# Two queues for the transfers of a feed-forward: moving the side traffic of the first gated ConvFFN from SyncE to GpSimd

## The chip, the cores and the metric

The kernel runs on one core of one Trainium2 chip. The time is the device time of one execution in microseconds (us). Engines: PE (TensorE), DVE (VectorE), ACT (ScalarE), POOL (GpSimd) and SP (SyncE, which here only issues transfers). Each engine runs its own instructions in order and waits on semaphores; a transfer that an engine issues stands in that engine's order like any other instruction.

## The reference, cut to what matters

One step of a two-layer encoder over 1024 prompt frames and 64 sample frames (1088 columns, width 1024). Layer 0 mixes with windowed attention, layer 1 with an S5 state-space model; each is followed by a gated convolutional feed-forward of width 2816:

```
def conv_ffn(h, prev, w_up, conv_w, conv_b, w_down):
    up = h @ w_up                                   # (t, 2*2816)
    full = concat([prev, up])                       # two rows of history
    c = conv_b + sum_j conv_w[j] * full[:, j:j+t]   # causal, width 3
    y = (gelu(c[..., :2816]) * c[..., 2816:]) @ w_down
    return y, full[:, -2:]

for i in range(2):
    x = x + rms_norm(mixer_i(rms_norm(x, g_pre_mix[i])), g_post_mix[i])
    x = x + rms_norm(conv_ffn(rms_norm(x, g_pre_ffn[i]), ...), g_post_ffn[i])
```

All is float32 at the interface. The state-space mixer of layer 1 needs tables made of its parameters alone (powers of the discretised poles, input and output matrices, a Toeplitz kernel per group); they depend on no activation and can be made at any time before layer 1.

## The kernel before, in words

Activations lie with the width on the 128 partitions and time along the rows, in three blocks of 384, 384 and 320 columns. A float32 product is three PE products of split operands (`mm3`, lines 235 to 237: low part times weight, high part times weight, high part times the weight's low part). A weight piece of 128x1024 is loaded by SP into a place called `raw` (line 196 or 213), and split by ACT and DVE into a `whl` tile (lines 198/199 and 227); `raw` has four places, `whl` six.

The first feed-forward (`ffn(0, ...)`) goes over 22 pairs of unit tiles (a gate tile and a value tile of 128 units each). A unit tile is 72 products, about 12 us of PE: three blocks `mm` of 24 products in PSUM, each read by DVE into `u` (lines 427, 429). ACT and DVE then do the convolution (`t`, lines 435 to 437), the gate is applied (line 453), and the gated pair goes to `gd` in DRAM (lines 454, 455). The down products that follow use a seven-product scheme, so they need sums of four quarters of the down weights and of the gated units. These are made beside the up-projection: `sums_w(k)` loads two pieces of `w_down` into the tile `jt` (line 368), makes four sums on DVE (371 to 374) and stores them to `sd` (375); `sums_g(k)` loads the pairs k and k+11 of `gd` into `jt` (380), makes four sums (383, 387 to 389) and stores them to `td` (390).

After each unit tile comes an `aside`: it lets one step of the side work run, and then the sums that are due by the table `starts`. The side work (`ssm_prep`) makes the tables of layer 1, in a small part and eight chunks (0 to 7). A chunk makes `ct` on DVE (lines 1055 to 1060, through the scratch tile `m`, one place), the product `w` on DVE (902 to 907 with DVE as engine), `kps` on PE (eight small products from `ct`, line 1083, each a pair in the trace), `kt` from it (1087, 1088), transposes `wps` of `w` on PE (1097) copied to `b3` (1098), a table `tab` on POOL (902 to 907 with POOL as engine, then 1106; it uses `m` too), and by way of the scratch `kd` in DRAM a Toeplitz tile `tl` (eight small loads, line 1118) and `tp` (1121). What is made is stored to `prm` (lines 1064, 1099, 1108, 1122).

The order on each engine is not the order of the code. A scheduler with a simulated timeline takes the recorded instructions, whose priority follows the place in the program, and side work has a lower one; what it decides is then fixed, and the engines run it in order. So an edit of which engine issues a transfer, or of which step it belongs to, can move any instruction near it.

Around the edit: up to the change all of these transfers but the tables' (line 1108) are issued by SP, in one order with the weight loads. In the second feed-forward (`ffn(1, ...)`), the same `sums_w`, `sums_g` and stores of `gd` are already issued by POOL, through tiles called `jw` and `jg`.

Of the kernel before, what the change touches and what calls it, by code (L numbers as in the profile page):

```python
# [8 lines left out]
F32 = mybir.dt.float32  # L9
# [6 lines left out]
P = 128  # L16
D = 1024
# [17 lines left out]
KH = KF // 2  # L35
# [8 lines left out]
class Core:  # L44
# [138 lines left out]
    def load_unit(self, src):  # L183
        nc = self.nc
        raw = self.wts.tile([P, D], F32, name="raw", tag="raw", bufs=4)
# [167 lines left out]
    def ffn(self, i, h, rb, after, side=None, beside=lambda: None, x=None, g=None):  # L353
# [10 lines left out]
        E, Q = nc.vector, (nc.sync, nc.gpsimd)[i]  # L364
# [12 lines left out]
        def sums_g(k):  # L377
            x = jt[:, :1536] if i == 0 else ts.tile([P, 1536], F32, name="jg", tag="t2")
            x = x.rearrange("p (c b t) -> p c b t", c=2, b=2)
            Q.dma_start(x, gd[:, k::KH, :768].rearrange("p c (b t) -> p c b t", b=2))  # L380
            yield
            a11, a12, a21, a22 = x[:, 0, 0], x[:, 0, 1], x[:, 1, 0], x[:, 1, 1]
            v = E.tensor_sub(a11, a12, a11)
# [11 lines left out]
        starts.update({2 * (k + KH) + 3 - i: sums_g(k) for k in range(KH)})  # L395
        jobs = {}

        def sums(j):
# [638 lines left out]
    def ssm_chunk(self, q):  # L1037
# [26 lines left out]
        nc.sync.dma_start(self.prm[:, gs, OC:OC + 256], oc.rearrange("p g c i t -> p g (c i t)"))  # L1064
# [6 lines left out]
        w = self.jt[:, 2048:].rearrange("p (g c j s) -> p g c j s", g=4, c=2, j=16)  # L1071
# [17 lines left out]
        nc.sync.dma_start(self.kd[q * P:q * P + P, 7:].rearrange("j t i -> j (t i)"), kt)  # L1089
# [9 lines left out]
        nc.sync.dma_start(self.prm[:, gs, OW:OW + 256], b3.rearrange("p g c n -> p g (c n)"))  # L1099
# [10 lines left out]
    def ssm_toeplitz(self, q):  # L1110
# [11 lines left out]
        nc.sync.dma_start(self.prm[:, 4 * q:4 * q + 4, OKT:OKT + 256], tp.rearrange("p (g e) f -> p g (e f)", e=2))  # L1122
# [105 lines left out]
    def ssm(self, after):  # L1228
# [4 lines left out]
        with tc.tile_pool(name="ss", bufs=1) as sp:  # L1233
# [36 lines left out]
            def batch(qs):  # L1270
# [11 lines left out]
                if e0 == 0:  # L1282

                    sc = self.wts.tile([P, D], F32, name="sc", tag="raw", bufs=4) if t < 8 or t == 9 else self.yp.tile([P, D], F32, name="sc", tag="ypA", bufs=2)
# [348 lines left out]
```

## Time and profile before

| | |
|---|---|
| runs | 2238.78, 2240.88, 2244.19 us; median 2240.88 |
| profiled execution | 2242.71 us, span 2240.9 us, mean clock of PE 0.989 |
| PE busy | 2192.9 us, 98% of the span |
| DVE busy | 1656.4 us, 74% |
| ACT, POOL busy | 1041.0 us, 46%; 410.0 us, 18% |
| first up-projection | about 383 to 929 us of the span |
| down products of layer 0 | about 929 to 1120 us |

The groups of the profile show what waits: ACT's splits wait for PE to free a `whl` place, PE hardly ever waits for a weight.

```profile
L227 ACT ACTIVATE whl<-raw 128x1024 fp32r<-128x1024 f32 x201 | 210.4, 1057 | 220.1 <-PE mm L237 193.7
L235 PE MATMUL mm<-hl,whl 128*128 128x384 f32 (+1 forms) x1960 | 643.7, 329 | 5.9 <-DVE hl L319 4.0
```

A line of this kind is a group of instructions: line, engine, operation, tile written and tiles read, count, then busy us and mean ns, then the engine's idle time just before them and what ended most of it.

### The profile page before, as it was taken

What the parts mean: (1) busy time and instruction counts of PE and PEld (TensorE: products, weight loads), DVE (VectorE), ACT (ScalarE), POOL (GpSimd) and SP (SyncE); (2) the same over time, 40 slices, a digit from 0 to 9 for tenths busy, and PEclk for the clock granted to TensorE, in tenths of its full rate; (3) what the DMA queues carried; (4) which work ended last, traced back from release to release, by engine and by line L of the source; (5) the groups of instructions that cost most, each with busy time, mean ns of one, the idle gap of its engine ahead of it and who ended that gap; (6) DMA issues with size and microseconds to landing.
All of it is one profiled execution on the core that took longest, in us unless ns stands there. A gap on an engine that the chain in (4) does not pass through costs nothing. (4 is left out here: it accounts for less than half of the span.)

```text
span 2240.9 us, 35962 instructions
## 1 busy us (share of the span) xinstructions
PE 2192.9 (98%) x13875; PEld 2119.2 (95%) x13875; DVE 1656.4 (74%) x2887; ACT 1041.0 (46%) x1895; POOL 410.0 (18%) x470
## 2 busy tenths in 40 slices
PE   9999999999999999999999899999999999999997
PEld 8987799999999999999996799999999999999997
DVE  8688648999778777766768855598976777677764
ACT  6256756322243333555545642263554445455553
POOL 5222005100032423100200034352010110100000
PEclk9999999999999999999999899999999999999999
DMA  6000015655245655886749988652266786578772
GB/s 221 32 30 21 20 62 170 229 212 201 95 147 181 191 184 167 285 290 212 240 154 342 284 282 301 239 167 75 91 233 216 260 274 208 194 252 316 224 267 73
DMA packets 208123, 428.47 MB, mean 191 GB/s; under 512 B 23312, under 2 KB 114224, under 8 KB 205008
## 3 DMA queue, kind: packets, MB, share of 16 engines
q1 hardware_dynamic: 175648, 326.56, 43.0%
q0 software_dynamic: 23984, 95.12, 11.9%
q10 hardware_dynamic: 8320, 4.49, 0.9%
q8 instruction: 109, 1.79, 0.3%
q14 instruction: 62, 0.51, 0.1%
HBM read 297.75 MB, written 128.37 MB: 190 GB/s over the span
## 5 line engine op out<-in xcount | busy, mean ns | idle before, releaser
L235 PE MATMUL mm<-hl,whl 128*128 128x384 f32 (+1 forms) x1960 | 643.7, 329 | 5.9 <-DVE hl L319 4.0
L236 PE MATMUL mm<-hh,whl 128*128 128x384 f32 (+1 forms) x1960 | 644.2, 329 | 0.0
L237 PE MATMUL mm<-hh,whl 128*128 128x384 f32 (+1 forms) x1960 | 642.8, 329 | 0.6 <-DVE whl L227 0.5
L235 PEld LDWEIGHTS mm<-hl,whl 128*128 128x128 f32 x1960 | 369.3, 189 | 8.1 <-DVE hl L319 4.9
L237 PEld LDWEIGHTS mm<-hh,whl 128*128 128x128 f32 x1960 | 369.3, 189 | 1.5 <-DVE whl L227 0.8
L236 PEld LDWEIGHTS mm<-hh,whl 128*128 128x128 f32 x1960 | 369.5, 189 | 0.2
L227 DVE TENSOR_TENSOR whl<-raw,whl 128x1024 fp32r<-128x1024 f32 x201 | 254.9, 1275 | 99.5 <-ACT whl L227 97.0
L235 PE MATMUL mm<-gt,whl 128*128 128x384 f32 (+1 forms) x968 | 316.4, 327 | 0.1
L236 PE MATMUL mm<-gt,whl 128*128 128x384 f32 (+1 forms) x968 | 316.0, 327 | 0.0
L237 PE MATMUL mm<-gt,whl 128*128 128x384 f32 (+1 forms) x968 | 315.5, 326 | 0.0
L227 ACT ACTIVATE whl<-raw 128x1024 fp32r<-128x1024 f32 x201 | 210.4, 1057 | 220.1 <-PE mm L237 193.7
L235 PEld LDWEIGHTS mm<-gt,whl 128*128 128x128 f32 x968 | 181.7, 188 | 0.4 <-DVE y L626 0.4
L236 PEld LDWEIGHTS mm<-gt,whl 128*128 128x128 f32 x968 | 181.7, 188 | 0.0
L237 PEld LDWEIGHTS mm<-gt,whl 128*128 128x128 f32 x968 | 181.7, 188 | 0.0
L199 DVE TENSOR_TENSOR whl<-raw,whl 128x1024 fp32r<-128x1024 f32 x84 | 95.7, 1152 | 54.0 <-ACT whl L198 53.9
L436 DVE SCALAR_TENSOR_TENSOR t<-u,ppt,t 128x1090 f32<-128x1090 f32 x88 | 126.2, 1435 | 5.5 <-ACT t L435 4.9
L435 ACT ACTIVATE t<-u,ppt 128x1090 f32<-128x1090 f32 x88 | 114.1, 1297 | 23.4 <-DVE u L532 13.0
L437 DVE SCALAR_TENSOR_TENSOR t<-u,ppt,t 128x1090 f32<-128x1090 f32 x88 | 123.3, 1403 | 0.5
L198 ACT ACTIVATE whl<-raw 128x1024 fp32r<-128x1024 f32 x84 | 82.2, 984 | 88.8 <-PE mm L237 88.0
L427 DVE TENSOR_TENSOR u<-rb,mm 128x384 f32<-128x384 f32 (+1 forms) x164 | 80.9, 503 | 47.8 <-PE mm L237 41.5
L576 DVE TENSOR_TENSOR gt<-gr,gt 128x768 fp32r<-128x768 f32 (+2 forms) x106 | 89.8, 872 | 27.9 <-ACT gt L575 27.6
L575 ACT ACTIVATE gt<-gr 128x768 fp32r<-128x768 f32 (+2 forms) x106 | 78.4, 771 | 53.1 <-DMA gr<-gd 24.7
(390 smaller groups left out, 4109.7 us busy)
## 6 DMA issues: line engine op xcount, KB each, us to landing
raw<-in_w_up SPq DMA_DIRECT2D x88, 512.0 KB, 4.4
raw<-in_w_down SPq DMA_DIRECT2D x74, 512.0 KB, 4.8
raw<-sd SPq DMA_DIRECT2D x40, 512.0 KB, 4.6
sj<-in_w_up POOLq DMA_DIRECT2D x68, 256.0 KB, 6.1
su<-sj POOLq DMA_DIRECT2D x34, 512.0 KB, 5.9
raw<-su SPq DMA_DIRECT2D x34, 512.0 KB, 3.8
pm<-prm SPq DMA_DIRECT2D x32, 522.0 KB, 7.7
gr<-td SPq DMA_DIRECT2D x40, 384.0 KB, 6.2
```

Source lines behind the costliest of these rows:

```text
L198: nc.scalar.activation(w[:, 0], raw, AF.Copy)
L199: nc.vector.tensor_sub(w[:, 1], raw, w[:, 0].bitcast(F32))
L227: x = nc.scalar.activation(w[:, 0], raw, AF.Copy), nc.vector.tensor_sub(w[:, 1], raw, w[:, 0].bitcast(F32))
L235: nc.tensor.matmul(out, w[:, 0, sl], xl, start=start, stop=False, skip_group_check=more)
L236: nc.tensor.matmul(out, w[:, 0, sl], xh, start=False, stop=False, skip_group_check=more)
L237: self.last_mm = nc.tensor.matmul(out, w[:, 1, sl], xh, start=False, stop=stop, skip_group_check=more)
L427: nc.vector.tensor_mul(u[:, t0 + 2:t0 + 2 + np_], rb[:, t0:t0 + np_], ps[:, :np_])
L435: nc.scalar.activation(t, u[:, 0:T + 2], AF.Identity, bias=cb(m), scale=cw(0, m))
L436: nc.vector.scalar_tensor_tensor(t, u[:, 1:T + 3], cw(1, m), t, op0=ALU.mult, op1=ALU.add)
L437: self.last_conv = nc.vector.scalar_tensor_tensor(t, u[:, 2:T + 4], cw(2, m), t, op0=ALU.mult, op1=ALU.add)
L575: nc.scalar.activation(x[:, 0, u], raw, AF.Copy)
L576: nc.vector.tensor_sub(x[:, 1, u], raw, x[:, 0, u].bitcast(F32))
```

## The change

Three things are edited.

1. In `ffn(0)` the queue `Q` is GpSimd's instead of SyncE's. The loads and stores of `sums_w` and `sums_g` and the stores to `gd` are issued by POOL, and in `ssm_chunk` and `ssm_toeplitz` so are the stores to `kd` and `prm` and the loads of `tl`. In all 185 transfers leave SP. The weights, the inputs of the norms and layer 1's loads stay on SP.
2. `sums_g(k)` loads at aside 2(k+11)+2 instead of 2(k+11)+3, and its sums are made two asides after the load instead of one. Two of them can now be under way, so they use the two halves of `jt` in turn; the tile `w` of the chunks, which lay in the third part of `jt`, gets a tile of its own.
3. `raw` (and the tile `sc` of layer 1, which has the same tag) has three places instead of four. The room goes to `w`.

```
-        raw = self.wts.tile([P, D], F32, name="raw", tag="raw", bufs=4)
+        raw = self.wts.tile([P, D], F32, name="raw", tag="raw", bufs=3)
...
-        E, Q = nc.vector, (nc.sync, nc.gpsimd)[i]
+        E, Q = nc.vector, nc.gpsimd
...
         def sums_g(k):
-            x = jt[:, :1536] if i == 0 else ts.tile([P, 1536], F32, name="jg", tag="t2")
+            x = jt[:, k % 2 * 1536:k % 2 * 1536 + 1536] if i == 0 else ts.tile([P, 1536], F32, name="jg", tag="t2")
...
-        starts.update({2 * (k + KH) + 3 - i: sums_g(k) for k in range(KH)})
+        starts.update({2 * (k + KH) + 2: sums_g(k) for k in range(KH)})
         jobs = {}
         def sums(j):
...
             if j in starts:
                 x = starts[j]
                 next(x)
-                jobs[j + 1 + i] = [x]
+                jobs.setdefault(j + 1 + (i or j > 2 * KH), []).append(x)
...
         if q == 0:
-            nc.sync.dma_start(self.kd[:, 0:7].rearrange("(b p) t i -> p b (t i)", p=P), z)
+            nc.gpsimd.dma_start(self.kd[:, 0:7].rearrange("(b p) t i -> p b (t i)", p=P), z)
...
-        nc.sync.dma_start(self.prm[:, gs, OC:OC + 256], oc.rearrange("p g c i t -> p g (c i t)"))
+        nc.gpsimd.dma_start(self.prm[:, gs, OC:OC + 256], oc.rearrange("p g c i t -> p g (c i t)"))
...
-        w = self.jt[:, 2048:].rearrange("p (g c j s) -> p g c j s", g=4, c=2, j=16)
+        w = self.prep2.tile([P, 4, 2, 16, 8], F32, name="w")
...
-        nc.sync.dma_start(self.kd[q * P:q * P + P, 7:].rearrange("j t i -> j (t i)"), kt)
+        nc.gpsimd.dma_start(self.kd[q * P:q * P + P, 7:].rearrange("j t i -> j (t i)"), kt)
...
-        nc.sync.dma_start(self.prm[:, gs, OW:OW + 256], b3.rearrange("p g c n -> p g (c n)"))
+        nc.gpsimd.dma_start(self.prm[:, gs, OW:OW + 256], b3.rearrange("p g c n -> p g (c n)"))
...
         for s in range(8):
-            nc.sync.dma_start(dst, src)
+            nc.gpsimd.dma_start(dst, src)
...
-        nc.sync.dma_start(self.prm[:, 4 * q:4 * q + 4, OKT:OKT + 256], tp.rearrange("p (g e) f -> p g (e f)", e=2))
+        nc.gpsimd.dma_start(self.prm[:, 4 * q:4 * q + 4, OKT:OKT + 256], tp.rearrange("p (g e) f -> p g (e f)", e=2))
```

The scheduler then sets another order at many places. Three are shown. The first is DVE at the start of the up-projection, where the last block's normed input is split into `hl` (line 319; the numbers behind names tell tiles apart, `jt` is the tile of the weight sums). Before:

```order
L372 TENSOR_TENSOR jt_4586<-jt_4586 128x512
L302 TENSOR_TENSOR nvsqb_3937<-nvsqb_3937 128x3
L344 TENSOR_TENSOR q_512<-q_512,xl_3847 128x640
L265 TENSOR_TENSOR sqb_3972<-sqb_3972,sqb_3974 128x640
L373 TENSOR_TENSOR jt_4586<-jt_4586 128x512
L303 TENSOR_TENSOR nvsqb_3937<-nvsqb_3937 128x3
L319 SCALAR_TENSOR_TENSOR hl_3949<-q_512,ppt_91,hh_3948 128x320 x2
L374 TENSOR_TENSOR jt_4586<-jt_4586 128x512
```

and with the change:

```order
L372 TENSOR_TENSOR jt_4586<-jt_4586 128x512
L302 TENSOR_TENSOR nvsqb_3937<-nvsqb_3937 128x3
L265 TENSOR_TENSOR sqb_3972<-sqb_3972,sqb_3974 128x640
L373 TENSOR_TENSOR jt_4586<-jt_4586 128x512
L303 TENSOR_TENSOR nvsqb_3937<-nvsqb_3937 128x3
L344 TENSOR_TENSOR q_512<-q_512,xl_3847 128x640
L374 TENSOR_TENSOR jt_4586<-jt_4586 128x512
L304 SCALAR_TENSOR_TENSOR nvsqb_3937<-nvsqb_3937 128x3
L319 SCALAR_TENSOR_TENSOR hl_3949<-q_512,ppt_91,hh_3948 128x320
L265 TENSOR_TENSOR sqb_3972<-sqb_3972,sqb_3977 128x640
L319 SCALAR_TENSOR_TENSOR hl_3949<-q_512,ppt_91,hh_3948 128x320
```

The last weight sum L374 stood behind the two last `hl`, and now stands ahead of them.

The second is DVE at the eighth chunk's `ct` (chunk 7), from the gated sum L383 on. Before:

```order
L383 TENSOR_TENSOR jt_4586<-jt_4586 128x384
L1055 TENSOR_TENSOR m_7019<-tq_4274,tp_4275 128x576
L1056 TENSOR_TENSOR m_7019<-tq_4274,tp_4275 128x576
L436 SCALAR_TENSOR_TENSOR t_8639<-u_8556,ppt_91,t_8639 128x1090
L387 TENSOR_TENSOR jt_4586<-jt_4586 128x384
L427 TENSOR_TENSOR u_8654<-rb_3688,mm_8657 128x384
L1057 TENSOR_TENSOR ct_7018<-m_7019 128x4x144
L437 SCALAR_TENSOR_TENSOR t_8639<-u_8556,ppt_91,t_8639 128x1090
```

and with the change, somewhat later in the program:

```order
L427 TENSOR_TENSOR u_8766<-rb_3688,mm_8803 128x384
L388 TENSOR_TENSOR jt_4586<-jt_4586 128x384
L1055 TENSOR_TENSOR m_7026<-tq_4274,tp_4275 128x576
L1056 TENSOR_TENSOR m_7026<-tq_4274,tp_4275 128x576
L389 TENSOR_TENSOR jt_4586<-jt_4586 128x384
L1057 TENSOR_TENSOR ct_7025<-m_7026 128x4x144
L1058 TENSOR_TENSOR m_7026<-tq_4274,tp_4275 128x576
L1059 TENSOR_TENSOR m_7026<-tq_4274,tp_4275 128x576
L427 TENSOR_TENSOR u_8774<-rb_3688,mm_8829 128x384
L1060 SCALAR_TENSOR_TENSOR ct_7025<-m_7026 128x4x144
```

The chunk's `ct` stood right behind L383, the first operation on the loaded gated units; now two blocks of `u` and most of the sums stand between. On PE the first `kps` of this chunk stood after the 20th product of `mm_8795`, with one product between each two; now it stands here, after the 18th product of `mm_8855`, and the other seven follow 14 products later, in `mm_8881`, without a product between:

```order
L236 MATMUL mm_8855<-hh_3897,whl_8561 128x384
L237 MATMUL mm_8855<-hh_3897,whl_8561 128x384
L1083 MATMUL kps_7148<-ct_7025,bd_4569 128x128
L235 MATMUL mm_8855<-hl_3898,whl_8561 128x384
L236 MATMUL mm_8855<-hh_3897,whl_8561 128x384
```

and

```order
L235 MATMUL mm_8881<-hl_3898,whl_8660 128x384
L236 MATMUL mm_8881<-hh_3897,whl_8660 128x384
L1083 MATMUL kps_7148<-ct_7025,bd_4569 128x128 x7
L237 MATMUL mm_8881<-hh_3897,whl_8660 128x384
L235 MATMUL mm_8881<-hl_3898,whl_8660 128x384
```

The third is POOL in the up-projection, at one chunk's table. Before:

```order
L902 TENSOR_TENSOR m_5814<-tq_4274,tp_4275 128x576
L903 TENSOR_TENSOR m_5814<-tq_4274,tp_4275 128x576
L904 TENSOR_TENSOR tab_5813<-m_5814 128x4x144
L905 TENSOR_TENSOR m_5814<-tq_4274,tp_4275 128x576
L906 TENSOR_TENSOR m_5814<-tq_4274,tp_4275 128x576
L907 TENSOR_TENSOR tab_5813<-m_5814 128x4x144
```

and with the change:

```order
L903 TENSOR_TENSOR m_5818<-tq_4274,tp_4275 128x576
L380 DMA jt_4586<-gd0_4001 128x2x768
L1118 DMA tp_4275<-kd_295 16x8x128 x8
L904 TENSOR_TENSOR tab_5817<-m_5818 128x4x144
L1099 DMA prm_294<-b3_5803 128x4x256
L390 DMA td0_4003<-jt_4586 128x1536
L905 TENSOR_TENSOR m_5818<-tq_4274,tp_4275 128x576
L906 TENSOR_TENSOR m_5818<-tq_4274,tp_4275 128x576
L1122 DMA prm_294<-tp_6065 128x4x256
L454 DMA gd0_4001<-t_7677 128x1024
L455 DMA gd0_4001<-t_7677 128x64
L907 TENSOR_TENSOR tab_5817<-m_5818 128x4x144
```

The table's six operations stood together; now 14 transfers stand among them behind its second one, each of which waits for what it reads.

More of the change, by code (lines that the diff above doesn't have):

```diff
@@ L1282, in batch @@
                 if e0 == 0:
-                    sc = self.wts.tile([P, D], F32, name="sc", tag="raw", bufs=4) if t < 8 or t == 9 else self.yp.tile([P, D], F32, name="sc", tag="ypA", bufs=2)
+                    sc = self.wts.tile([P, D], F32, name="sc", tag="raw", bufs=3) if t < 8 or t == 9 else self.yp.tile([P, D], F32, name="sc", tag="ypA", bufs=2)
                     tiles[t] += [sc[:, :552].rearrange("p (e c k) -> p e c k", e=2, c=2), sp.tile([P, 2, 2, 138], F32, name="rd", bufs=2)]
```

## The prediction, made before the change was run

> **What bounds the kernel now.** I read the page first, then PE by stage, then who PE waits for in the changed stage, and last the timelines around each wait.
>
> ```profile
> span 2240.9 us, 35962 instructions
> 350.00:560.00 210.00, 204.53 (x1238) 203.27 (x1237) 193.12 (x475) 81.47 (x134) 35.40 (x25) 0.98 0.61 215
> 560.00:850.00 290.00, 290.00 (x1811) 289.56 (x1810) 230.12 (x367) 105.51 (x149) 79.53 (x56) 1.00 0.50 161
> 850.00:930.00 80.00, 75.30 (x452) 74.57 (x451) 54.69 (x82) 28.31 (x40) 22.97 (x17) 0.96 0.64 210
> 930.00:1120.00 190.00, 190.00 (x1127) 189.91 (x1127) 137.54 (x176) 105.10 (x141) 14.84 (x11) 1.00 0.75 253
> ```
>
> A row is a stretch: its length, then the busy time of PE, PEld, DVE, ACT and POOL, and the granted clock of PE before the DMA share. The first feed-forward's up-projection lies between about 383 and 929 us. PE is the bound: it has no idle time at all from 560 to 850 and from 930 to 1120. Nothing that the change does there can gain; it can only lose. What can be won is PE's 5.5 us before 560, its 4.7 us after 850, and the time in which its clock was low.
>
> ```profile
> PE kps L1083 <- DVE ct L1060: 3.9, 1, 3.9
> PE mm L235 <- DVE hl L319: 3.7, 2, 2.4
> PE mm L235 <- DVE u L427: 1.8, 1, 1.8
> PE kps L1083 <- DVE ct L1057: 0.8, 1, 0.8
> 400.00:405.00 5.00, 4.11 (x18) 4.11 (x19) 4.20 (x9) 0.74 (x1) 1.95 (x2) 0.67 0.90 353
> 435.00:440.00 5.00, 5.00 (x20) 5.00 (x21) 5.00 (x10) 2.51 (x4) 0.00 (x0) 0.66 0.26 88
> 885.00:890.00 5.00, 5.00 (x22) 5.00 (x23) 5.00 (x10) 2.17 (x4) 0.00 (x0) 0.52 0.82 296
> ```
>
> These are all of PE's waits from 350 to 930 us (total, times, longest), and the stretches behind them. Each wait but the shortest is followed by some 3 to 5 us of low clock, so a wait costs itself and a slow stretch. I call them A (400 us, for `hl`), B (435 us, for `u`) and C (880 to 890 us, for the eighth chunk's `ct`). (The Trainium skill, "TensorE: Matmul & The Clock Gate", Part 1, has the clock halved after an idle window of about 3.4 us and restored after as long a busy one; the rows agree on the length of the slow stretch, but B shows it after 1.8 us.)
>
> C comes from a transfer:
>
> ```profile
> 869.73 0.57 SPq L380 DMA_DIRECT2D jt<-gd  x1
> 875.25 0.56 DVE L383 TENSOR_TENSOR jt<-jt 128x384 f32<-128x384 f32 x1 [10.11 <-DMA jt<-gd]
> 875.72 0.75 DVE L1055 TENSOR_TENSOR m<-tq,tp 128x576 f32<-128x576 f32 x1
> 876.39 0.75 DVE L1056 TENSOR_TENSOR m<-tq,tp 128x576 f32<-128x576 f32 x1
> 883.93 0.75 DVE L1060 SCALAR_TENSOR_TENSOR ct<-m 128x576 f32<-128x576 f32 x1
> 840.40 0.34 PE L235 MATMUL mm<-hl,whl 128*128 128x384 f32 x1
> 840.57 0.38 PE L1083 MATMUL kps<-ct,bd 128*128 128x128 f32 x2
> 840.97 0.38 PE L1083 MATMUL kps<-ct,bd 128*128 128x128 f32 x2
> 880.16 0.46 PE L1083 MATMUL kps<-ct,bd 128*128 128x128 f32 x2 [0.76 <-DVE ct L1057]
> 884.74 0.80 PE L1083 MATMUL kps<-ct,bd 128*128 128x128 f32 x2 [3.94 <-DVE ct L1060]
> 889.66 0.48 PE L235 MATMUL mm<-hl,whl 128*128 128x384 f32 x1
> ```
>
> The load of the gated units goes out on SP at 869.73, behind the stores it needs. DVE, in order, stands 10.1 us at L383; all of the chunk's work is queued behind it. DVE then works without a gap, but `ct` is done at 884.7, and PE has stood for it twice.
>
> **The change part by part.** Sums are made against the profiled execution, 2242.7 us (span 2240.9 and 1.8 around it); it lies 1.8 above the runs' median of 2240.88, so I take differences and set them against the median.
>
> *C goes.* The waits are 0.76 + 3.94 = 4.70. From 884.74 to 889.66 PE runs seven groups (a pair of `kps` and one product) in 4.92; in the chunk before, a group took 840.97 - 840.57 = 0.40, so seven are 2.8 and 2.1 are lost to the clock, with 0.2 at the ends. C is 7.0 in all. In the new order the load L380 is issued half a pair earlier, L383 stands behind a later `u`, and the first `kps` stands 13 rows later on PE, with the other seven 14 products behind it. A product of 384 columns takes 0.17 (840.40 to 840.57). From the end of `mm_8829`, the last block that DVE reads before L1060, to the seven `kps` there are 18 + 14 products, 5.5 us. DVE at that point: from the end of `mm_8803` it has L427, L388, L1055, L1056, L389, L1057, L1058, L1059, by the spacing in C's own timeline (875.25 to 875.72, 0.47, for a short one, and to 876.39, 0.67, for one of 576 elements) 3 x 0.47 + 5 x 0.67 = 4.8, against 24 x 0.17 = 4.2 for `mm_8829`; then L427 and L1060, 1.2. `ct` is done about 1.8 after `mm_8829` and wanted at 5.5: 3.7 us of room, where before it was 3.9 late. Should DVE come late by the whole room, C comes back step for step. C: -7.0, bounds -7.0 and 0.
>
> *A grows.* DVE's rows where its second wait (2.4 us) ends:
>
> ```profile
> 400.10 1.20 DVE L319 SCALAR_TENSOR_TENSOR hl<-q,ppt,hh 128x320 fp32r<-128x320 f32 x2
> 401.22 1.35 DVE L374 TENSOR_TENSOR jt<-jt 128x512 f32<-128x512 f32 x1
> ```
>
> The new order puts L374 ahead of the two last L319, so `hl` for k=4 comes 1.3 later: +1.3 here, bounds 0 (L374 took 0.68 where POOL did not compute beside it) and +2.5 (a longer slow stretch). POOL's third `hl` now stands behind L375, which waits for L374; PE wants it about 5 us after that, with the k=4 to 6 products and eight of the next unit before it, so it is hidden.
>
> *B shrinks a little.* `jt` has one place for the weight sums: store, load, sum.
>
> ```profile
> 415.66 0.33 SPq L375 DMA_DIRECT2D sd<-jt  x1
> 424.07 0.39 SPq L368 DMA_DIRECT2D jt<-in_w_down  x1
> 430.49 0.69 DVE L371 TENSOR_TENSOR jt<-jt 128x512 f32<-128x512 f32 x1 [0.38 <-DMA jt<-in_w_down]
> sd<-jw POOLq DMA_DIRECT2D x11, 1024.0 KB, 4.9
> jw<-in_w_down POOLq DMA_DIRECT2D x11, 1024.0 KB, 6.2
> gd<-t SPq DMA_DIRECT2D x21, 512.0 KB, 2.6
> gd<-t POOLq DMA_DIRECT2D x22, 512.0 KB, 4.5
> ```
>
> On SP the load waited 4 us behind a weight load. On POOL, with the landing times that the same transfers have in the second feed-forward, it lands at 415.7 + 0.5 + 4.9 + 0.7 + 6.2 = 428.0, so the 0.38 goes, and three small operations (0.3) have moved behind `u`: -0.7, bounds 0 and -3.5 (the 1.8 and its slow stretch, 5 x 0.34 = 1.7, all gone).
>
> *The moved transfers.* 185 issues leave SP and enter POOL's queue:
>
> ```profile
> L375 POOL DMA_DIRECT2D sd<-jw x11: 532/549/565, 1642.1 to 1828.5; - x11
> L1108 POOL DMA_DIRECT2D prm<-tab x16 | 12.4, 775 | 3.2 <-POOL tab L1106 3.1
> L907 POOL TENSOR_TENSOR tab<-m 128x576 f32<-128x576 f32 x8 | 16.0, 1998 | 0.6
> POOL m L902 <- DVE jt L907: 364.0, 8, 182.6
> ```
>
> One costs 0.55 to 0.78 of POOL where it cost SP 0.33 (415.66). A chunk (some 40 us: 840.57 to 880.16) brings eight L1118, four other small ones and about seven of the gated units: 19 x 0.55 = 10.5 to 19 x 0.78 = 15, besides the table's 12 us (six operations of up to 2.0). POOL sat idle 364 us waiting for the chunks before, so it has the time. What is queued behind a waiting issue is the table (L904 to L907), and the next chunk's L1055 on DVE needs it done, since both use `m`. In chunk 7 I count from DVE's w (its L907): L902 and L903, two issues, the wait for `b3` some 7 us on, two issues, then four operations of about 1.75: done near 15 us, against L1055 at about 23. For other chunks POOL may hold DVE by up to 3 us, about the room of their `kps`. I set 0, bounds 0 and +6 (one more event like C).
>
> *Three raw places and the second half of `jt`.* A weight piece must be loaded into the place of the third before it:
>
> ```profile
> 936.38 1.04 ACT L198 ACTIVATE whl<-raw 128x1024 fp32r<-128x1024 f32 x1
> 938.96 2.35 DVE L199 TENSOR_TENSOR whl<-raw,whl 128x1024 fp32r<-128x1024 f32 x2
> 946.28 1.06 ACT L198 ACTIVATE whl<-raw 128x1024 fp32r<-128x1024 f32 x1 [2.20 <-PE mm L237]
> raw<-in_w_down SPq DMA_DIRECT2D x22, 512.0 KB, 4.8
> ```
>
> The piece split at 936.38 is free at 940.2; the third after it is split at 946.28, which is 6.1 later, and a load lands in 4.8. ACT waited there for PE, not for the load. In the up-projection pieces come about 12 us apart. Nothing, therefore; if that cover went, the split would move by what is missing, behind six `whl` places.
>
> Sum: -7.0 + 1.3 - 0.7 = -6.4; 2240.9 - 6.4 = 2234.5 (2236.3 for an execution like the profiled one).
>
> **The rivals.**
>
> *C only moves* (no measurable change). DVE leaves the wait for `jt<-gd` and stands at L1055 or L1057 for POOL instead, with `kps` late again. For it: L1055 to L1060 are in the same order behind POOL's table, and POOL's queue has got longer. Against it: the room of 3.7 and of 8 us above. If half of C stays and A grows, 2240.9 - 3.5 + 1.3 = 2238.7; all of it, 2242.2.
>
> *POOL's queue is the new bound* (slower). One in-order queue now holds stores that wait for DVE, loads that wait for stores, and tables that DVE waits for. Each L380 stands for a `gd` store's landing, 4.5 on POOL against 2.6, and L907 stands behind them. If that makes L1055 late by more than about 3.7 in two chunks that lost nothing before, each costs a C without its first wait, 3.9 + 2.3 = 6.2: 2240.9 - 6.4 + 12.4 = 2246.9. It decides once POOL is held some 8 us longer per chunk than I count. Against it: 364 us of slack. (The Trainium skill speaks for it: "DMA: Bandwidth & Descriptors", SWDGE vs HWDGE vs iDMA, leaves plain transfers to SP or ACT, and "SBUF — State Buffer", the "DVE blocks DMA" trap, has GpSimd's descriptors starved while DVE runs certain copies. The rows of the second feed-forward show landings of up to 6.2 us on POOL and a store later by 1.9, no queue that stops.)
>
> *All three waits go* (larger gain). If the later weight sums also free DVE at A and B: 7.0 + 3.5 + 4.0 for A's second wait and its clock (2.4 and 5 x 0.33), 2240.9 - 14.5 = 2226.4. Against it, L374 ahead of `hl`.
>
> **How the numbers follow.** Forecast 0.50, C only moves 0.26, POOL's queue 0.16, all go 0.08. This kernel's measurement tells 0.2%, 4.5 us, from no change. The forecast lies only 1.9 beyond it, so a tenth of its chance falls within: faster 0.45 + 0.08 and 0.01 of the first rival = 0.54; same 0.05 + 0.25 = 0.30; slower 0.16. The range takes in the larger gain's near side and the slower case's: 2228 to 2246; the forecast's own, from its bounds, is 2231 to 2238.
>
> **What would show it.** Right: PE's waits from 350 to 930 have no `kps` row, 850 to 930 is busy for the whole of its length at clock 1.00, and DVE's wait at L383 is near nothing. A's wait is near 3.7 rather than 2.4. Wrong: a `kps` wait with DVE standing at L1055 or L1057 for POOL L907 or for the store of `b`; a low clock between 560 and 850; splits of ACT waiting for raw loads after 930.

## The result and the profile after

The changed kernel takes 2254.11 us (median of 5 runs, 2249.62 to 2256.09), the kernel before 2240.88 beside it: ratio 1.0057, 95% interval 1.0044 to 1.0069. It is slower by 13, where 6 less were forecast, and 8 above the range. Run a second time, it took 2249.88 against 2243.18 (ratio 1.0037, 1.0023 to 1.0052). Two single executions, one of the kernel before (9453 us) and the profiled one of r3_tabst below (3044 us at a granted clock of 0.65), are left out of all ratios.

Two stretches of the changed kernel that were shown of before (length; busy PE, PEld, DVE, ACT, POOL; PE's granted clock; DMA share), with two at the start of the down products:

```profile
560.00:850.00 290.00, 290.00 (x1805) 289.65 (x1804) 230.70 (x349) 104.38 (x148) 135.94 (x164) 1.00 0.50 171
850.00:930.00 80.00, 75.40 (x470) 74.95 (x469) 62.77 (x84) 29.17 (x40) 45.97 (x53) 0.98 0.62 198
925.00:930.00 5.00, 0.93 (x3) 0.96 (x4) 2.03 (x3) 2.39 (x4) 0.00 (x0) 0.70 1.05 379
930.00:935.00 5.00, 5.00 (x21) 5.00 (x20) 5.00 (x9) 4.53 (x7) 0.65 (x2) 0.62 0.65 225
```

and PE's waits from 350 to 930 us (total, times, longest):

```profile
PE mm L235 <- DVE gt L576: 4.6, 1, 4.6
PE mm L235 <- DVE u L427: 2.6, 1, 2.6
PE mm L235 <- DVE hl L319: 2.4, 1, 2.4
PE mm L235 <- DVE u L429: 0.8, 1, 0.8
```

Both `kps` rows are gone: C went. A new row stands first, the wait for `gt`, the split of the gated units that the first down products take. It ends at 929, and the clock is low to 935. So 850 to 930 has no more busy time than before, for another reason. The transfers of the eighth chunk on the way to C, now:

```profile
869.66 0.77 POOL L380 DMA_DIRECT2D jt<-gd  x1
881.63 0.55 DVE L383 TENSOR_TENSOR jt<-jt 128x384 f32<-128x384 f32 x1
889.22 0.75 DVE L1060 SCALAR_TENSOR_TENSOR ct<-m 128x576 f32<-128x576 f32 x1
889.80 0.38 PE L1083 MATMUL kps<-ct,bd 128*128 128x128 f32 x2
892.45 1.72 PE L1083 MATMUL kps<-ct,bd 128*128 128x128 f32 x14
```

L380 goes out at the same time as before (869.7), but DVE comes to L383 late enough to find it landed, and no `kps` waits. What changed is where the work stands: the chunk's first `kps` comes 9.6 later than before (880.16), of which this execution was 2.5 behind, and `ct` is done at 890.0, 2.5 before the other seven `kps`.

To see where the rest went I compare the start of the same matrix product, by its place in PE's order, in two profiled executions. The differences of the changed kernel to the one before, in us gained or lost per stretch (marks are times of the kernel before):

```
stretch             first profile   second profile
start to 700 (A, B)      +2.5           +0.5
700 to 905 (C)           -7.5           -7.5
905 to 945 (gt)          +7.0           +6.7
945 to 1530              +4.9           +2.5
1530 to 1820             +2.9           +2.5
1820 to the end          +1.2           +0.7
sum                     +11.0           +5.4
```

C gave its whole gain; the start of the down products took it back; and 6 to 9 us more were lost after 945, in stages in which the change moves no transfer. PE's waits from 950 to 2300 us, before:

```profile
PE p L1281 <- DMA pm<-prm: 3.1, 3, 2.0
PE pr L279 <- DVE sqa L273: 1.7, 1, 1.7
PE p L1341 <- ACT ys L1355: 1.5, 1, 1.5
PE mm L235 <- DVE u L531: 1.5, 2, 1.1
```

and with the change:

```profile
PE p L1281 <- DMA pm<-prm: 6.2, 3, 4.0
PE mm L235 <- DVE u L531: 5.4, 5, 1.4
PE pr L279 <- DVE sqa L273: 3.9, 2, 2.2
PE p L1341 <- ACT ys L1355: 2.8, 1, 2.8
```

The four together are 18.3 against 7.8, and with the rows not shown, some of which fell, 28.5 against 22.7: the later loss is spread over several stages.

### The profile page after: what moved, and what is told of

It reads as the page before. It is cut to its first block, busy times and chain, and to the rows that moved or that the text cites. A ratio compares the mean times of both kernels' runs of the same rounds, so it can differ in the third digit from the quotient of the medians.

```text
span 2252.3 us, 36013 instructions
## 1 busy us (share of the span) xinstructions
PE 2197.9 (98%) x13875; PEld 2122.1 (94%) x13875; DVE 1667.4 (74%) x2887; ACT 1040.7 (46%) x1895; POOL 513.7 (23%) x655
## 5 line engine op out<-in xcount | busy, mean ns | idle before, releaser
L227 DVE TENSOR_TENSOR whl<-raw,whl 128x1024 fp32r<-128x1024 f32 x201 | 258.2, 1291 | 103.1 <-ACT whl L227 102.4
L199 DVE TENSOR_TENSOR whl<-raw,whl 128x1024 fp32r<-128x1024 f32 x84 | 98.9, 1186 | 56.9 <-ACT whl L198 56.8
L436 DVE SCALAR_TENSOR_TENSOR t<-u,ppt,t 128x1090 f32<-128x1090 f32 x88 | 127.9, 1455 | 6.5 <-ACT t L435 5.7
L437 DVE SCALAR_TENSOR_TENSOR t<-u,ppt,t 128x1090 f32<-128x1090 f32 x88 | 127.3, 1448 | 0.8
L344 POOL TENSOR_TENSOR y<-y,xl 128x768 f32<-128x768 f32 (+1 forms) x16 | 30.2, 1888 | 327.9 <-DVE y L341 263.4
```

Source lines behind the costliest of these rows:

```text
L199: nc.vector.tensor_sub(w[:, 1], raw, w[:, 0].bitcast(F32))
L227: x = nc.scalar.activation(w[:, 0], raw, AF.Copy), nc.vector.tensor_sub(w[:, 1], raw, w[:, 0].bitcast(F32))
L344: x = by[q].tensor_add(yq, yq, xs[q])
L436: nc.vector.scalar_tensor_tensor(t, u[:, 1:T + 3], cw(1, m), t, op0=ALU.mult, op1=ALU.add)
L437: self.last_conv = nc.vector.scalar_tensor_tensor(t, u[:, 2:T + 4], cw(2, m), t, op0=ALU.mult, op1=ALU.add)
```

## The experiments

Two questions: what makes `gt` late at 925, and what costs after 945? In the table each row is one profiled execution against the first one of before, by the same stretches, and the ratio of all its runs to those of before on its chip. "Tables" are the six transfers of the parameter chunks (L1045, L1064, L1089, L1099, L1118, L1122), "stores" the gated units' L454 and L455, "sums" L368, L375, L380 and L390; named are those that POOL issues in the first feed-forward.

```
run         on POOL                  to 700  C      gt    later  ratio (95%)
change      all                      +2.5   -7.5   +7.0   +9.0   1.0057 (1.0044-1.0069)
r1_after    all (again)              +0.5   -7.5   +6.7   +5.6   1.0037 (1.0023-1.0052)
e2_queue    all, old start of sums   +1.6   -7.5   +3.6   +7.8   1.0077 (1.0059-1.0095)
e3_raw4     all, four raw places     +0.9   -7.4   +3.7  +10.1   1.0071 (1.0054-1.0088)
e8_gr       all and L587             -0.5   -7.5   +2.1  +13.1   1.0028 (1.0015-1.0041)
t1_pad8     all, 8 copies            -0.7   -7.5   +6.1   +1.3   1.0034 (1.0020-1.0048)
e7_prepsp   stores, sums, shifted    +3.6   -7.5    0.0   +9.0   1.0009 (0.9995-1.0023)
e6_sums     stores, sums             +2.2   -7.5    0.0   +8.7   1.0038 (1.0022-1.0054)
e10_tabst   tables, stores           +1.0   -7.5    0.0   +7.8   1.0014 (1.0000-1.0027)
e9_tabsums  tables, sums              0.0   -7.5    0.0   +3.1   0.9995 (0.9985-1.0005)
r4_tabsums  tables, sums (again)     -1.5   -7.5    0.0   +3.1   1.0004 (0.9990-1.0018)
t2_pad31    tables, sums, 31 copies  -0.3   -7.5    0.0   +4.7   1.0008 (0.9996-1.0021)
e5_prep     tables                   -0.7   -7.5    0.0   +1.9   0.9978 (0.9966-0.9990)
e1_raw3     none, three raw places   -3.5   -3.2    0.0   +2.2   0.9993 (0.9983-1.0004)
e4_shift    none, shifted sums       -1.7   +6.2    0.0   +0.1   1.0029 (1.0018-1.0040)
d1_dummy    88 more stores           -3.8  +11.2   +0.3   +2.3   1.0063 (1.0039-1.0086)
d2_dummy    44 more stores           -3.9   +2.5   +0.2   +1.7   1.0040 (1.0025-1.0055)
r2_before   none (before again)      -1.2   -0.1    0.0   -0.3   0.9996 (0.9987-1.0005)
```

### The parts of the change

Three raw places alone:

```
-  raw = self.wts.tile([P, D], F32, name="raw", tag="raw", bufs=4)
+  raw = self.wts.tile([P, D], F32, name="raw", tag="raw", bufs=3)
   (and the same for sc)
```

> The kernel before with three raw places instead of four and nothing else (all transfers still on SP, sums as before). Theory (the loss is the third edit: SP issues weight loads in order, a load that waits for its raw place holds every load behind it on SP): the eighth chunk's wait for kps stays, and the losses seen behind 905 us come: a wait for gt at the start of the down products (about +7 with its slow clock), the state-space and GLU stage (+2 to +4), the second feed-forward (+3 to +6): 2251 to 2258 us. Rival (the loss comes from GpSimd's transfers, by their descriptors or their queue): 2239 to 2244 us.

2238.29 against 2239.33: no cost. The first theory after the result, that the third place was needed, fell.

The queue alone, with the old start of the sums, four raw places and one place of `jt`:

```
-  E, Q = nc.vector, (nc.sync, nc.gpsimd)[i]
+  E, Q = nc.vector, nc.gpsimd
   (and nc.sync to nc.gpsimd in the six transfers of the tables)
```

> The first edit alone: the 185 transfers issued by GpSimd, sums_g at its old asides in one part of jt, w in jt, four raw places. Theory (raw places are the loss): nothing is lost behind 930 us; the load L380 no longer stands behind SP's weight loads, so part of the eighth chunk's wait (7.0) goes, the wait B grows by about 2.5: 2235 to 2242 us. Rival (GpSimd's transfers are the loss): 2248 to 2256 us.

2257.99 (2248.65 to 2260.78; the profiled execution is the lowest of them). The whole loss is in this part of the change: C goes, `gt` is waited for, and the later stages lose.

The change with four raw places; one place of `jt` for the gated sums, `w` in `jt`:

```
-  raw = self.wts.tile([P, D], F32, name="raw", tag="raw", bufs=3)
+  raw = self.wts.tile([P, D], F32, name="raw", tag="raw", bufs=4)
   (and the same for sc)
-  w = self.prep2.tile([P, 4, 2, 16, 8], F32, name="w")
+  w = self.jt[:, 2048:].rearrange("p (g c j s) -> p g c j s", g=4, c=2, j=16)
```

> The change with four raw places: w back in the last third of jt, so the gated sums use one place of jt in turn instead of two; queue and asides as in the change. Theory (raw places are the loss): the eighth chunk's kps waits are gone (-7), B +2.5, nothing behind 930 us: 2234 to 2238 us. Rival (GpSimd's transfers are the loss): 2248 to 2256 us.

2253.13: the fourth raw place gives nothing back.

The shift of the gated sums alone, everything on SP:

```
-  starts.update({2 * (k + KH) + 3 - i: sums_g(k) for k in range(KH)})
+  starts.update({2 * (k + KH) + 2: sums_g(k) for k in range(KH)})
-  jobs[j + 1 + i] = [x]
+  jobs.setdefault(j + 1 + (i or j > 2 * KH), []).append(x)
```

> The second edit alone: the gated sums loaded half a pair earlier and made two asides after the load, in one place of jt, all transfers on SP, four raw places. Theory: the kps waits of the eighth chunk go by the shift alone: 2233 to 2237 us. Rival (it takes the queue on GpSimd to have the load out early): the 10 us wait at L383 stays, 2239 to 2243 us.

2244.73, ratio 1.0029. The shift does not remove C by itself; it gives more such waits. PE's in the up-projection:

```profile
PE kps L1083 <- DVE ct L1060: 6.5, 3, 3.5
PE kps L1083 <- DVE ct L1057: 3.4, 1, 3.4
```

### What the queue does: each family by itself

The tables' transfers alone go to POOL:

```
-  nc.sync.dma_start(dst, src)
+  nc.gpsimd.dma_start(dst, src)
   (L1118; the same in L1045, L1064, L1089, L1099 and L1122)
```

> The kernel before with only the tables' transfers (L1045, L1064, L1089, L1099, L1118, L1122: 105 issues) on POOL's queue; the gated units' stores and the sums stay on SP, in the old order. Theory (order of transfers): POOL's last table, L906, stands behind the last chunk's eight L1118 and so frees the place for gr<-gd late: the down products begin with a wait for gt of 3 to 5 us (none before), +3 to +4 from 905 to 945 us; C stays about as large as before or gets a little smaller. Theory (later landings): jw<-in_w_down lands about 0.5 us later than before's 6.2 and the second feed-forward loses 3 to 6 us; in all 2245 to 2251. Rival (only the sums and stores carry the loss): no gt wait, second feed-forward as before, 2238 to 2243.

2234.2 against 2238.85, faster by 0.10 to 0.34%: the best of all kernels here, and against both theories, as it has no `gt` wait and loses only 1.9 later. C is gone with the sums still on SP and at their old start. The rows of the last gated unit that the load needs show why. Its operations are L436, L437 and L453 on DVE, then the stores L454 and L455. Before:

```profile
852.29 5.62 SPq L1118 DMA_DIRECT2D tp<-kd  x8
854.12 2.27 DVE L436 SCALAR_TENSOR_TENSOR t<-u,ppt,t 128x1090 f32<-128x1090 f32 x1
857.49 2.36 POOL L907 TENSOR_TENSOR tab<-m 128x576 f32<-128x576 f32 x1
858.95 2.06 DVE L453 TENSOR_TENSOR t<-t 128x1090 f32<-128x1090 f32 x1
861.99 0.38 SPq L1122 DMA_DIRECT2D prm<-tp  x1
862.46 1.86 SPq L454 DMA_DIRECT2D gd<-t  x1
869.73 0.57 SPq L380 DMA_DIRECT2D jt<-gd  x1
```

and with the tables' transfers on POOL:

```profile
850.38 4.18 POOL L1118 DMA_DIRECT2D tp<-kd  x8 [1.61 <-DMA kd<-kt]
850.56 1.35 DVE L436 SCALAR_TENSOR_TENSOR t<-u,ppt,t 128x1090 f32<-128x1090 f32 x1 [0.32 <-ACT t L435]
853.69 1.29 DVE L453 TENSOR_TENSOR t<-t 128x1090 f32<-128x1090 f32 x1
855.00 0.32 SPq L454 DMA_DIRECT2D gd<-t  x1
858.43 0.53 SPq L380 DMA_DIRECT2D jt<-gd  x1
```

The load goes out 11.3 earlier. Only 1.4 of this is SP's queue: the eight L1118 were through before the unit was made (L453 ends at 861.0), and its store then stood behind L1122 until 862.5. Another 6.0 come from DVE, where L453 now ends at 855.0. L436, L437 and L453 took 2.27, 2.15 and 2.06 before, while POOL computed its table beside them, and take 1.35, 1.36 and 1.29 here, while POOL is mostly issuing transfers; that is 2.5, and the rest is the place in DVE's order. The last 3.8 lie between store and load, which waits for the landing (7.3 before, 3.4 here). DVE's order behind the load moved too: L1055 stood right behind L383, and now comes 8 after it. So moving the tables' transfers removes C, but less by freeing SP's queue than by what it changes on POOL, on DVE and in the landing; no run changes these one at a time.

Only the sums and the stores go to POOL, old start:

```
-  E, Q = nc.vector, (nc.sync, nc.gpsimd)[i]
+  E, Q = nc.vector, nc.gpsimd
```

> The kernel before with only the gated units' stores and the two kinds of sums on POOL's queue (80 issues in the first feed-forward); the tables' transfers stay on SP, the start of the sums is unchanged. Theory (order of transfers): no gt wait at the start of the down products, because POOL's tables have no L1118 ahead of them. C: the load of the gated units goes out in the same place, but its store lands 1.9 us later (4.5 against 2.6), so C stays or grows by 2. Theory (later landings, by number of transfers): 80 of 185 moved, the second feed-forward loses some 2 to 3 us; in all 2241 to 2248. Rival: landings do not depend on what went before, second feed-forward as before, 2239 to 2243.

2246.33, no `gt` wait, C gone as well; but later +8.7. The change with the tables' transfers back on SP (shift, three raw places and the second half of `jt` stay):

```
-  nc.gpsimd.dma_start(dst, src)
+  nc.sync.dma_start(dst, src)     (and the other five)
```

> The change with the six tables' transfers back on SP; the sums and stores on POOL, the shift of the sums, three raw places and the second half of jt stay. Theory (order of transfers): C is gone (-7 by 905 us), no gt wait of more than 1 us at 925, so 945 stands at -4 to -7 against before, where the whole change stands at +2; the rest loses 2 to 4 in the second feed-forward if the earlier transfers set its landings: 2235 to 2242. Rival (any GpSimd transfer near the tables makes gr late): gt wait of 3 to 5 again and 2245 to 2252.

2241.47, not to be told from before; no `gt` wait. (Its profiled execution, the +9.0 of the table, is the slowest of its twelve, 2248.23.) So neither family makes `gt` late by itself. Of the later loss I thought that it grows with what has gone through POOL's queue before. That was tried by 88 more stores of 256 KB from POOL in the first feed-forward, to a piece of DRAM that nobody reads (it shifts the addresses of later ones):

```
+  [nc.gpsimd.dma_start(dum[:, f, j], ta[:, 128 * j:128 * j + 512])
+   for j in range(4)]              (behind L455, first feed-forward)
```

> The kernel before with 88 more POOL stores of 256 KB in the first feed-forward (four a pair), to a piece of DRAM that nobody reads; they add no work for the later stages, whose instructions keep their order on every engine. (The piece of DRAM moves the addresses of later ones.) Theory (what went through POOL's queue earlier sets later landings): jw<-in_w_down lands later than 6.2 by 0.5 or more, and the second feed-forward is 4 to 8 us longer than before though nothing in it changed: 2244 to 2252. Rival (landings depend on what runs at the time): the second feed-forward within 1 us of before, landings 6.2 to 6.4; whatever is lost is lost before 930 us.

2253.06, but the loss lies before 905 us, in three `kps` waits (11.9 in all); later +2.3, like the 2.2 of e1_raw3. That theory fell.

### Which order makes gt late

The change again, unaltered:

> The changed kernel once more, unaltered, for a second profiled execution. What belongs to the program stands again at the same place: C gone (905 us at -4 to -6 against before), the wait for gt of 3 to 5 with its slow stretch (+6 to +7 from 905 to 945), waits A and B together +2 to +3. Theory that the later losses belong to the program too: +4 at 1440 us and +1 to +3 in the second feed-forward come again, span 2250 to 2255. Rival (they are chance of one execution): they come at other places or not at all.

The `gt` wait is 4.5 and C -7.5 again; the later loss is 5.6 instead of 9.0, with nothing at 1440, where 4 had gone. The change with the first gated loads on POOL:

```
-  nc.sync.dma_start(r[:, :n], gd[:, 6 * x:6 * x + n, :384])
+  (nc.gpsimd, nc.sync)[i].dma_start(r[:, :n], gd[:, 6 * x:6 * x + n, :384])
```

> The change with one edit: the first two loads of gated units for the down products (L587, first feed-forward) are issued by POOL, right behind the last table, instead of by SP, where they stand behind two weight loads that hold the queue for 7 us. Theory (the loss at 925 us is this queue position): the loads go out near 915 instead of 917 to 924 and land by 920; the wait for gt falls from 4.6 to below 1, 945 us stands at -3 to -5 against before instead of +2, and the whole is 5 to 7 faster than the change: 2246 to 2249. Rival (the last table itself is what is late, whoever issues): gt wait stays above 3, 2252 to 2256.

The rows of SP, POOL and PE around the first gated loads L587 (`gr`); they need the place of the last chunk's tables, so L906. Before:

```profile
899.00 1.17 POOL L906 TENSOR_TENSOR m<-tq,tp 128x576 f32<-128x576 f32 x1
907.74 2.70 SPq L587 DMA_DIRECT2D gr<-gd  x2
912.96 4.65 SPq L196 DMA_DIRECT2D raw<-in_w_down  x2
```

with the change:

```profile
909.57 7.12 SPq L196 DMA_DIRECT2D raw<-in_w_down  x2
910.55 2.22 POOL L906 TENSOR_TENSOR m<-tq,tp 128x576 f32<-128x576 f32 x1
916.87 1.04 SPq L587 DMA_DIRECT2D gr<-gd  x2
927.09 2.31 ACT L575 ACTIVATE gt<-gr 128x768 fp32r<-128x768 f32 x3 [5.26 <-DMA gr<-gd]
929.07 0.66 PE L235 MATMUL mm<-gt,whl 128*128 128x384 f32 x1 [4.60 <-DVE gt L576]
```

and with L587 on POOL:

```profile
907.34 2.22 POOL L906 TENSOR_TENSOR m<-tq,tp 128x576 f32<-128x576 f32 x1
911.98 1.74 POOL L587 DMA_DIRECT2D gr<-gd  x2
918.75 2.31 ACT L575 ACTIVATE gt<-gr 128x768 fp32r<-128x768 f32 x3
```

and PE's wait there in this kernel:

```profile
PE mm L235 <- DVE gt L576: 1.9, 1, 1.9
```

In the changed order two weight loads L196 stand ahead of L587 on SP, and before they stood behind it. They hold SP until 916.7, four after L906 is done at 912.8, and the DMA engines are full while the last loads land (share 1.05 from 925 to 930). Off that queue, L587 goes out 2.4 after L906's end, the split begins 8 earlier (3 of it because this execution was ahead by then), and the stretch loses 2.1 instead of 6.7 to 7.0. The wait goes with the program's order: in the five profiles with L196 ahead (change, r1_after, e2_queue, e3_raw4, t1_pad8) PE waits 3.3 to 4.6 for `gt`, in all those with L587 ahead not at all. But the last table is late in the same five: L906 ends at 909.4 to 912.8 there, and at 908.0 at the latest in those without the wait. In the change its operations L902 to L906 take 14.7 us on POOL (898.1 to 912.8) with eleven transfers among them, before 7.2. With L587 off SP's queue PE still waits 1.9 of the 4.6. So 2.7 are shown for the two weight loads; the 1.9 stand with the late table, which no run moved by itself. It takes all three families on POOL to get that order, which two further kernels show. Tables and sums, stores on SP:

```
   before, with nc.gpsimd in the tables' six transfers
-  Q.dma_start(...)           (L368, L375, L380, L390)
+  nc.gpsimd.dma_start(...)
```

> The kernel before with the tables' transfers and those of the sums (L368, L375, L380, L390) on POOL; the gated units' stores (L454, L455) stay on SP; old start of the sums. Tables alone gave 2234.2, all three kinds together 2258.0. Theory (any wait in the one queue that the tables share with the sums makes the last table late): gt wait of 3 to 5 at 925, 2246 to 2256. Rival (it is the 44 stores in the queue, which wait for the gated units): no gt wait, 2234 to 2243.

Tables and stores, sums on SP:

```
   before, with nc.gpsimd in the tables' six transfers
-  Q.dma_start(gd[...], ta[...])           (L454, L455)
+  nc.gpsimd.dma_start(gd[...], ta[...])
```

> The kernel before with the tables' transfers and the gated units' stores (L454, L455) on POOL; the sums' transfers stay on SP. Theory (any wait in the queue that the tables share makes the last table late): stores wait for the gated unit, up to 9 us each, so gt wait of 2 to 5 and 2240 to 2250; L380 on SP waits 1.9 longer for a store that lands in 4.5, so some of C may come back. Rival (only the sums matter, whose load waits for the store of the unit before it): no gt wait, 2232 to 2238.

Neither has a `gt` wait. In both the last table is done by 904.6 (L906 at 903.43 and 897.01), and L587 stands ahead of L196. For the whole time e8_gr gains nothing, though: 2249.83 beside 2249.88 of the unaltered change; its profiled execution lost 13.1 later. The `gt` wait is shown as a loss of its stretch; a gain of the whole from shortening it is not.

### What costs after 945

By now the kernels that store the gated units from POOL lost 5.6 to 13.1 after 945, those that do not 0.1 to 3.1. The pair e9_tabsums and e10_tabst is the sharpest: from about 1260 us on they have the same instructions in the same order on every engine. The second feed-forward of e9_tabsums, at one weight sum:

```profile
1663.20 0.71 POOL L368 DMA_DIRECT2D jw<-in_w_down  x1 [5.06 <-DMA sd<-jw]
1668.26 0.55 POOL L454 DMA_DIRECT2D gd<-t  x1 [4.35 <-DVE t L453]
1668.96 0.69 DVE L371 TENSOR_TENSOR jw<-jw 128x512 f32<-128x512 f32 x1 [0.99 <-DMA jw<-in_w_down]
```

and of e10_tabst, whose products there run 0.9 ahead of it:

```profile
1666.66 0.71 POOL L368 DMA_DIRECT2D jw<-in_w_down  x1 [6.72 <-DMA sd<-jw]
1667.41 0.56 POOL L454 DMA_DIRECT2D gd<-t  x1
1676.61 0.69 DVE L371 TENSOR_TENSOR jw<-jw 128x512 f32<-128x512 f32 x1 [9.50 <-DMA jw<-in_w_down]
```

The store before lands later, so the load goes out with the gated store right behind it, and DVE stands 9.5 instead of 1.0 for it; `u` comes late and PE waits 4.7. In this execution the chain of store, load and sum has grown a small delay into a wait of PE. Was it chance, or the kernel? Before, e10_tabst and e9_tabsums again, unaltered, and before with 44 more POOL stores in the gated stores' own shapes:

```
+  [nc.gpsimd.dma_start(dum[:, f, o:e], ta[:, o + (2 if o else 0):e + (2 if o else 0)])
+   for o, e in ((0, SEQ), (SEQ, T))]      (behind L455, first feed-forward)
```

> The kernel before once more, unaltered, for a second profiled execution. Theory (the loss of 2 to 7 us between 1530 and 1820 us belongs to kernels that store the first stage's gated units from POOL): none here, within 1 us of the first. Rival (chance of an execution, whatever the kernel): it may come here too, with a wait for u L531 of 2 to 5.

> The tables' transfers and the gated units' stores on POOL once more, unaltered. Its first profiled execution lost 6.3 in one wait for u L531 near 1690 us, where the load of a weight sum went out at the same time as a store and a weight load. Theory (belongs to the kernel): 2 to 7 lost again between 1530 and 1820. Rival (chance): 0 to 1, or at another k.

> The tables' and the sums' transfers on POOL once more, unaltered. From the middle of the gated stage on, its instructions and waits are the same, engine by engine, as those of the kernel with the stores instead of the sums. Theory (belongs to the stores): 1530 to 1820 within 1 of before, again. Rival (chance): 2 to 7 lost here this time.

> The kernel before, in which POOL also writes each gated unit of the first feed-forward, in the gated stores' own two shapes (44 more transfers), to a piece of DRAM that nobody reads; SP's own stores stay. Theory (stores of these shapes through POOL's queue do something that lasts): 2 to 7 lost between 1530 and 1820. Rival (no such thing): within 1 of before there; whatever is lost is lost before 930, at the waits for kps.

r2_before and r4_tabsums lost nothing from 1530 to 1820 (-1.3 and -2.2), nor did d2_dummy (+0.7): in this execution, more stores of these shapes on POOL did nothing that lasted. It is the fastest of d2_dummy's four, 2243.62; the other three took 2246.49 to 2250.14, and where they lost it is not known. r3_tabst has no profile that can be compared by stretch; its runs gave 1.0010 (0.9994 to 1.0025).

One thing differed at the head of that chain. The sum's last operation and its store, in before (second profile):

```profile
1640.56 0.69 DVE L374 TENSOR_TENSOR jw<-jw 128x512 f32<-128x512 f32 x1
1641.55 0.53 POOL L375 DMA_DIRECT2D sd<-jw  x1 [10.43 <-DVE u L409]
```

and with the change:

```profile
1648.01 0.69 DVE L374 TENSOR_TENSOR jw<-jw 128x512 f32<-128x512 f32 x1
1649.46 0.53 POOL L375 DMA_DIRECT2D sd<-jw  x1 [10.89 <-DVE u L409]
```

POOL issues 0.30 after the sum there and 0.76 here. Such late issues, always by 0.46, stand at the same transfers in repeats. In all five profiles in which the first store was late (e2_queue, e3_raw4, e10_tabst, and the change twice) this stage lost 2.5 to 7.2 (e7_prepsp lost 3.7 and e8_gr 2.1 without one). I took them to be places in POOL's own stream, and moved them by small copies on POOL, with every other engine's order kept: off the first store in the change (8 copies), onto it in e9_tabsums (31 copies).

```
+  [nc.gpsimd.tensor_copy(pad[:, j:j + 1], ta[:, j:j + 1]) for j in range(8)]
   (behind L455, second feed-forward, first pair; 31 spread over four pairs)
```

> The change with eight copies of one column added on POOL, behind the first gated unit's stores of the second feed-forward, where POOL is idle for over 10 us; every other engine's order is the same. Theory (at fixed places in its own stream POOL starts an instruction 0.46 us late, and in the change one of these places is the store of the first weight sum, from which the chain store, load, sum comes late and grows): the places move by eight instructions, to a gated store and to waits that are idle anyway; the first store goes out 0.3 behind the sum instead of 0.75, and the second feed-forward (1530 to 1820) stands within 1 of before, where the two profiles of the change lost 2.9 and 2.5. In all 1 to 4 less than the change. Rival (the place on POOL is not the cause): 2 to 4 lost again.

> The kernel with the tables' and the sums' transfers on POOL (second feed-forward -0.8 and -2.2 against before in its two profiles), with 31 copies of one column added on POOL in the idle times of the second feed-forward's first four pairs; every other engine's order is the same. By the count of POOL's instructions this puts a late place on the store of the first weight sum, as in the kernel with the stores, which lost 6.2. Theory: that store goes out 0.75 behind its sum instead of 0.29, and 2 to 6 are lost from 1640 to 1760. Rival (the place on POOL does nothing by itself): the store may go out late, but the stage stays within 1 of before.

Both fell. The late place did not move. With 8 copies the change's first store goes out 0.75 behind its sum (the sum ends at 1639.91, the store starts at 1640.66), and with 31 copies that of e9_tabsums 0.29 behind it (1638.82 and 1639.11), both as without the copies. And t1_pad8, with its late first store, lost nothing in the stage (-0.5) and 1.3 in all after 945: a late store is not enough. Its twelve runs fall into two groups, five from 2241.98 to 2243.83 and seven from 2248.12 to 2252.89; the profiled one (2242.2) is of the first.

What stands: nine profiles with the stores on POOL in place of SP lost 8.0 on average after 945 (1.3 to 13.1), nine without 2.1 (-0.3 to 4.7). That points at the stores and does not show them as the cause. Each number is one execution. From 945 to 1530 alone, the three profiles with tables and sums on POOL lost 3.8 to 5.7, those with the stores 0.1 to 9.2. And the ratios of the sharpest pair, 0.9995 and 1.0014, were 1.0004 and 1.0010 when both were run again, with intervals that overlap. No run moved the stores alone. The loss is not the same in each execution, and where it was followed up it came as the wait of a chain of transfers. What in the earlier stage makes it likelier is open.

## Why the prediction was wrong, point by point

*C goes* was right in size (-7.0, measured -7.5) and half right in its reason. I counted on the load half a pair earlier and on `ct` wanted later, with 3.7 of room. In the changed kernel `ct` is wanted later (the first `kps` stands 44 to 48 products further on in PE's records of its two profiles, more than the 13 rows I read), with 2.5 of room, but the load goes out at the same time as before. The new order is not the shift's doing: e2_queue loses the same 7.5 without the shift, and the shift alone gives more of these waits (+6.2, e4_shift). Nor does C need all of it to go: it goes by the same 7.5 in every kernel that takes any two of the three families, or the tables alone, off SP. I had read that L380 goes out "behind the stores it needs", and did not look at what made those stores late. In e5_prep, which has the load 11.3 earlier, 6.0 of that were DVE's work on the gated unit and 3.8 the landing, and only 1.4 SP's queue.

*A grows*, *B shrinks a little* (+1.3 and -0.7): the other way round in the rows. A's wait is 2.4 in all, where 3.7 was before and a longer one was forecast, and B's is 2.6 + 0.8, where 1.8 was before and 1.1 was forecast. The two profiles stand at +2.5 and +0.5 by 700, t1_pad8 at -0.7; the forecast of +0.6 is within what an execution changes there.

*The moved transfers*, set at 0, is the step that failed. I bounded it by what is queued behind a waiting issue inside the up-projection, the table and the next chunk's L1055, and there it held: no `kps` waits. I did not follow the last chunk, whose table holds the place that the first gated loads of the down products take and is done late (14.7 us for L902 to L906 instead of 7.2), nor see that the new order puts two weight loads ahead of these on SP. Together that costs 6.7 to 7.0 in the two profiles of the change, just over the upper bound of +6, and at a place where I had PE without idle time and only wrote that it could lose.

*Three raw places and the second half of `jt`*, at nothing: right for the raw places (0.9993, 0.9983 to 1.0004). The half of `jt` was only run together with others.

The sum took every stage after 930 as unchanged. That is the second step that failed, +5.6 and +9.0 in the two profiles, and its cause stays open.

Of the rivals, "POOL's queue is the new bound" had the sign and the queue, but its place (L1055 late, then `kps`) was wrong: in no profile with transfers of this stage moved to POOL does a `kps` wait. For the advice of the Trainium skill, "DMA: Bandwidth & Descriptors", SWDGE vs HWDGE vs iDMA, to leave plain transfers to SP or ACT, the runs go both ways: 105 moved transfers of the tables made the kernel faster (0.9978), all 185 together slower (1.0057).

## What to carry to other kernels

When a load is late, go back through the store that it needs to the operation that makes the data, and split the delay among the three before giving it to the queue: here the queue had 1.4 of 11.3. When transfers change queue, follow the last one of the stage to whoever takes its buffer next, and print the order of the other queues at that point, because a builder may reorder them. A chain of store, load and sum that already makes its reader wait can take back several us in one execution and none in the next, so a gain of a few us has to be measured in its own stretch, in more than one profile.

## What was not expected of the hardware

POOL issues a transfer 0.29 us after the event that releases it, but at some transfers 0.75. The places were the same in each repeat (the change twice, e9_tabsums twice), 16 transfers apart where two could be seen in a row (15 where the larger L380 was among them), and they stayed on the same transfers with 8 and 31 more instructions on POOL ahead of them. So they go by transfers and not by instructions; what they are is not shown. The same program differed by 3.4 us after 945 between two executions (the change), with C and `gt` alike to 0.3.
